# The attention stage's two extra projection weights move to another pool of on-chip memory

## The chip, the cores and the metric

The kernel runs on one core of one Trainium2 chip. The metric is the device time of one execution in microseconds (us), the median of several runs. The core has TensorE (PE in the rows; its weight loads are PEld), VectorE (DVE), ScalarE (ACT), GpSimd (POOL) and SyncE (SP), which issues the DMAs. Every engine takes its instructions in the order in which they stand in its list; semaphores hold an instruction until those it depends on are done.

## The reference

One decoder layer for 4096 prompt positions and 8 single-token samples. Both are projected by one matrix `w_in`; one half of the features goes through a convolution and a gated linear recurrence, the other through windowed attention with sinks. Both halves are gated, joined, and projected by `w_out`.

```python
xn = rms_norm(x, norm_pre)
proj = jnp.einsum('btd,de->bte', xn, w_in)
x_rnn, g_rnn, q, k, v, g_att = jnp.split(proj, SPLITS, axis=-1)
xc, new_conv = causal_conv(x_rnn, conv_state, conv_w, conv_b)
h, h_last = rg_lru(xc, h0, w_gate_a, b_gate_a, w_gate_x, b_gate_x, lru_lambda)
rnn_out = h * jax.nn.silu(g_rnn)
att = window_attention_prompt(q, k, v, attn_sinks, rel_bias)   # the samples: own keys and caches
mix = jnp.concatenate([rnn_out, att * jax.nn.silu(g_att)], axis=-1)
y = x + rms_norm(jnp.einsum('bte,ed->btd', mix, w_out), norm_post)
```

## The kernel before

The positions are cut into eleven chunks: chunk 0 has 256 positions and the 8 samples, chunks 1 to 10 have 384 each. The work goes in three stages. The **recurrent stage** (A) projects every chunk into the recurrence's input and gate (`pr`), forms two gates per block of 128 features on TensorE (`gt`, line 327), runs the scan on VectorE (`hh`, line 352), multiplies it with the SiLU gate (line 361) and stores it into the scratch `mix_d` (line 362). The scan of a chunk needs one square root over all four blocks (`uu`, line 348), for which ScalarE loads another activation table. The **attention stage** (B) projects the chunks again, now to K (`pk`), V (`pv`), four query tiles (`pq`) and four gate tiles (`pga`), each of 24 matmuls, and works through units of one head group and 128 queries: scores (`S`), softmax on VectorE and ScalarE (`tt`, lines 622 to 632), transposes (`pT`), splits (`ph`, `pl`, lines 639 and 640) and products with V (`po`). The **output stage** (C) reads `mix_d` and projects by `w_out`. The products run on values split in two parts (names with h and l), so that three matmuls make one.

**Memory.** Pools are stacked: the attention stage's pools begin where those of the recurrent stage began. The recurrent stage has `pa_late` (bytes 126,592 to 171,136 of each partition: `uu`, `sg`, `aa`, `hh` and others, used until its last instruction), above it `pa` (to 196,896: gate weights, `xk`, `thg`), and above that `prep` (to 220,000: the input rows `xs`). The attention stage has `pb_late` (126,592 to 173,184), `pb` (to 202,848: V `vs`, keys `kt`, softmax `tt`) and `pb1` (to 216,672: `vt`, queries `sq`). The first tile of a new pool that lies over old pools waits until all tiles of the old ones under the pool are released, those that it doesn't touch too; which instruction then carries this wait is seen in the built program.

**Weights.** The attention stage needs ten weight tiles of `w_in`. Eight take the slots of `wpool`; the ninth and tenth, gate tiles 2 and 3 (`wh_in` and `wl_in` 16 and 17), lie at the bottom of `pb_late`. Loading one means a 512 KB DMA into `ws`, a copy on ScalarE (line 111) and a subtraction on VectorE (line 112):

```python
ws = (spare or stage).tile([P, KD, P], F32, tag="ws", name=f"ws_{n}")
nc.sync.dma_start(ws, src)
wh = pool.tile([P, KD, P], F32R, tag="wh", name=f"wh_{n}", bufs=bufs)
act(wh, ws, AF.Copy)
eng.tensor_sub(wl, ws, wh)
```

**Order and PSUM.** The order on every engine is set at build time by a list scheduler that simulates the program and takes what it believes ready first; a wait that falls away or comes up shifts whole stretches. In the attention stage all projections share two PSUM banks (`ps_mm`, line 76); a projection can begin when one of them has been read out. K is read out into `kt` (lines 484, 486), a query tile into `sq` (lines 564 to 567) and, in chunk 0, `qz` (line 571).

Of the kernel before, what the change touches and what calls it, by code (L numbers as in the profile page):

```python
# [9 lines left out]
F32 = mybir.dt.float32  # L10
# [5 lines left out]
P = 128  # L16
# [4 lines left out]
NH = 8  # L21
# [3 lines left out]
NSAMP = 8  # L25
# [19 lines left out]
def hymba_kernel(ctx: ExitStack, tc: tile.TileContext, ins, outs):  # L45
# [69 lines left out]
    def load_w_in(m, pool=None, bufs=None, spare=None, eng=nc.vector, fast=False):  # L115
        return load_w(w_in_v[:, :, m * P:(m + 1) * P], f"in{m}", pool or wpool, bufs, spare, eng, fast)
# [81 lines left out]
    cms = [tc.tile_pool(name=n, bufs=1) for n in ("pa_late", "pa", "prep")]  # L198
# [217 lines left out]
    wB = {}  # L416
# [24 lines left out]
    for ci in range(NCH):  # L441
        for item in A_ORDER:
            f, s = item[0], st[ci]
            c = int(item[1:] or 0)
# [237 lines left out]
    def attend_sample(pool):  # L682
        def window(new, cache, dst, n):
            pr = ps_t(f"pr_{n}")
            nc.tensor.transpose(pr[:NSAMP, 0:P], new, ident)
            row = pbl.tile([NSAMP, P], F32, tag="sh", name=f"row_{n}", bufs=2)
            nc.vector.tensor_copy(row, pr[:NSAMP, 0:P])
            win = pbl.tile([P, NSAMP, P], F32, tag="wh", name=f"win_{n}", bufs=2)
            rows = cache[0].rearrange("b j v d -> j b (v d)")
            nc.sync.dma_start(win[0:112], rows[1:113])  # L690
            nc.sync.dma_start(win[112:P - 1], rows[113:P])
            nc.sync.dma_start(win[P - 1:P], row)
            nc.sync.dma_start(dst[0].rearrange("b j v d -> j b (v d)"), win)
            return win
# [1 line left out]
        kw = window(ksT, ck, o_ks, "k")  # L696
        vw = window(vsT, cv, o_vs, "v")
        yield
        kT = pbl.tile([P, NSAMP, P], F32, tag="wl", name="kT_s", bufs=2)
        for half in range(2):  # L700
            pt = ps_t(f"ptk_{half}")
            for b in range(4):
                nc.tensor.transpose(pt[:, b * P:(b + 1) * P], kw[:, half * 4 + b, :], ident)
            nc.vector.tensor_copy(kT[:, half * 4:half * 4 + 4].rearrange("p b k -> p (b k)"), pt)
        yield
        T = pbl.tile([P, NSAMP, P], F32, tag="wl", name="T_s", bufs=2)[:NH]
        for half, f in enumerate((ps_t, ps_v)):
            S = f(f"S_samp{half}")[:NH].rearrange("p (b k) -> p b k", k=P)
            for b in range(4):
                nc.tensor.matmul(S[:, b, :], qz[:, half * 4 + b, :], kT[:, half * 4 + b, :], start=True, stop=True)  # L710
            nc.vector.tensor_tensor(T[:, half * 4:half * 4 + 4], S,
                                    bs.rearrange("p (o k) -> p o k", o=1).broadcast_to([NH, 4, P]), op=ALU.add)
        m = pool.tile([NH, 4, NSAMP], F32, name="m_s")
        nc.vector.tensor_reduce(m[:, 0], T, axis=mybir.AxisListType.X, op=ALU.max)
        nc.vector.tensor_scalar(m[:, 1], m[:, 0], sk8, None, op0=ALU.max)
        nc.vector.tensor_sub(T, T, m[:, 1].rearrange("p (b o) -> p b o", o=1).broadcast_to([NH, NSAMP, P]))
        act(T, T, AF.Exp)
        nc.vector.tensor_reduce(m[:, 2], T, axis=mybir.AxisListType.X, op=ALU.add)
        act(m[:, 3], m[:, 1], AF.Exp, scale=-1.0, bias=sk8)
# [20 lines left out]
        n = chunks[0][1]  # L740
# [4 lines left out]
    phase[0] = "B"  # L745
    pcms = [tc.tile_pool(name=n, bufs=1, space=bass.MemoryType.PSUM) for n in ("psb0", "psb1", "psb2")]
    ps[:] = [c.__enter__() for c in pcms]
    cms = [tc.tile_pool(name=n, bufs=1) for n in ("pb_late", "pb", "pb1")]
    pbl, pb, pb1 = [c.__enter__() for c in cms]
    xB = load_x(0)  # L750
    for item in B_FIRST:
        if item[0] in "KVQG":
            m = {"K": 12, "V": 13, "Q": 8, "G": 14}[item[0]] + (int(item[1]) if item[0] in "QG" else 0)
            wB[m] = load_w_in(m) if len(wB) < 8 else load_w_in(m, pbl, 2)
    state = [{} for _ in chunks]
    state[0]["xs"] = xB
    work = [chunk_B(ci, state[ci], state[ci - 1]) for ci in range(NCH)]
    for ci in range(NCH):
        for item in B_ORDER if ci else B_FIRST:
            f, args = item[0], [int(i) for i in item[1:]]  # L760
# [10 lines left out]

    wC = [load_w_out(e) for e in range(8)]
    sample = attend_sample(pb)
    turn = 0

    order = [*range(1, NCH), 0]
    for ci in order:
# [14 lines left out]
        for j, (xsrc, ydst, rows, off) in enumerate(tiles):  # L792
            n = f"{ci}_{j}"
# [108 lines left out]
```

## Time and profile before

| | us |
|---|---|
| median of 3 runs (1443.89 to 1446.31) | 1444.59 |
| the profiled execution | 1450.88 |
| its span, first to last instruction | 1449.2 |
| TensorE busy in the span | 1403.5 |
| VectorE, ScalarE, GpSimd busy | 914.3, 800.0, 440.9 |
| last store of the recurrent stage issued | 511.56 |

TensorE is busy nearly without a gap except from 474 to 538 us, where chunk 10 of the recurrent stage and chunk 0 of the attention stage meet. A timeline row gives start, duration, engine, line, operation and operands, with the idle time before it in brackets and what ended it.

### The profile page before, as it was taken

To read this page: it belongs to the slowest core of one execution; us is meant where nothing else is said; L and a number is where in the kernel's file an instruction comes from. 1 tells how busy PE (TensorE), PEld (TensorE's weight loads), DVE (VectorE), ACT (ScalarE), POOL (GpSimd) and SP (SyncE) were. 2 spreads that over 40 slices of the span, in tenths; PEclk is the share of its full clock that TensorE was granted. 3 is DMA by queue.
4 is the path that set the end of the run, shared out by engine and by line. 5 is a ranking of instruction groups with operands and counts; after the bars stand their busy time and mean duration, and the time that the engine had idled before them with its cause. 6 is when DMAs were issued, how large, how long until landed. Compare 5 with 4: busy or idle time off the path is not lost.

```text
span 1449.2 us, 24120 instructions
## 1 busy us (share of the span) xinstructions
PE 1403.5 (97%) x8127; PEld 1323.5 (91%) x8127; DVE 914.3 (63%) x2258; ACT 800.0 (55%) x2055; POOL 440.9 (30%) x876
## 2 busy tenths in 40 slices
PE   5999999999999889999999999999999999999998
PEld 4999989999999779999999999999998888888886
DVE  6778877777777767557566566566784445334433
ACT  4566656665555656577676676576783222222211
POOL 3233332222421033354463453453543000000000
PEclk9999999999999999999999999999999999999999
DMA  9324453434236330330320320330444534433431
GB/s 274 133 83 157 149 168 138 153 131 139 97 121 196 90 117 22 119 106 12 110 99 12 110 99 12 109 99 12 162 133 146 167 134 142 145 133 133 147 129 60
DMA packets 115029, 170.23 MB, mean 117 GB/s; under 512 B 12215, under 2 KB 98823, under 8 KB 114907
## 3 DMA queue, kind: packets, MB, share of 16 engines
q1 hardware_dynamic: 114906, 168.71, 34.7%
q8 instruction: 64, 1.05, 0.3%
q14 instruction: 59, 0.48, 0.1%
HBM read 100.19 MB, written 68.50 MB: 116 GB/s over the span
## 4 chain that ended last, share of the span: by engine, by line
PE 68%; DVE 3%; ACT 2%; DMA 1%; issue 1%; SPq 0%; POOL 0%; POOLq 0%; DVEq 0%; ACTq 0%
PE out L819 8%; PE out L821 8%; PE out L820 8%; PE pga L122 4%; PE pga L123 4%; PE pga L124 4%; PE pq L123 4%; PE pq L122 4%; PE pq L124 4%; PE po L661 3%; PE S L601 2%; PE S L602 2%; PE pT L635 2%; PE pr L122 1%; PE pr L124 1%; PE pr L123 1%
## 5 line engine op out<-in xcount | busy, mean ns | idle before, releaser
L123 PE MATMUL pr<-xl,wh_in 128*128 128x384 f32 (+1 forms) x688 | 231.8, 338 | 0.0
L122 PE MATMUL pr<-xh,wh_in 128*128 128x384 f32 (+1 forms) x688 | 220.1, 340 | 10.8 <-ACT xc L302 10.8
L124 PE MATMUL pr<-xh,wl_in 128*128 128x384 f32 (+1 forms) x688 | 230.0, 336 | 0.0
L819 PE MATMUL out<-wh_out,xh_mix_d 128*128 128x512 f32 (+1 forms) x520 | 201.3, 387 | 0.0
L820 PE MATMUL out<-wl_out,xh_mix_d 128*128 128x512 f32 (+1 forms) x520 | 200.9, 386 | 0.0
L821 PE MATMUL out<-wh_out,xl_mix_d 128*128 128x512 f32 (+1 forms) x520 | 200.5, 386 | 0.0
L838 ACT ACTIVATE sqc<-out 128x512 bf16<-128x512 f32 (+2 forms) x67 | 39.2, 585 | 192.5 <-PE out L821 182.4
L122 PEld LDWEIGHTS pr<-xh,wh_in 128*128 128x128 f32 x688 | 129.9, 191 | 12.5 <-ACT xc L302 12.2
L627 ACT ACTIVATE tt<-tt,nm 128x129 f32<-128x129 f32 x256 | 100.0, 393 | 72.0 <-DVE nm L624 71.8
L841 DVE TENSOR_TENSOR out<-out,gpost 128x512 f32<-128x512 f32 (+1 forms) x65 | 45.4, 699 | 147.6 <-ACT sqc L838 147.0
L123 PEld LDWEIGHTS pr<-xl,wh_in 128*128 128x128 f32 x688 | 131.3, 191 | 0.7 <-issue 0.7
L124 PEld LDWEIGHTS pr<-xh,wl_in 128*128 128x128 f32 x688 | 131.1, 191 | 0.0
L122 PE MATMUL pq<-xh_B,wh_in 128*128 128x384 f32 (+1 forms) x352 | 117.7, 335 | 1.8 <-ACT qz L571 1.1
L123 PE MATMUL pga<-xl_B,wh_in 128*128 128x384 f32 (+1 forms) x352 | 118.8, 337 | 0.0
L122 PE MATMUL pga<-xh_B,wh_in 128*128 128x384 f32 (+1 forms) x352 | 117.7, 334 | 0.7 <-ACT qz L571 0.7
L123 PE MATMUL pq<-xl_B,wh_in 128*128 128x384 f32 (+1 forms) x352 | 118.0, 335 | 0.0
L124 PE MATMUL pq<-xh_B,wl_in 128*128 128x384 f32 (+1 forms) x352 | 117.8, 335 | 0.0
L124 PE MATMUL pga<-xh_B,wl_in 128*128 128x384 f32 (+1 forms) x352 | 117.2, 333 | 0.0
L141 POOL TENSOR_TENSOR rs_c<-ssc,mhalf 128x1 f32<-128x1 f32 (+1 forms) x33 | 20.5, 622 | 315.0 <-DVE ssc L842 276.1
L819 PEld LDWEIGHTS out<-wh_out,xh_mix_d 128*128 128x128 f32 x520 | 97.7, 188 | 19.9 <-issue 0.2
L821 PEld LDWEIGHTS out<-wh_out,xl_mix_d 128*128 128x128 f32 x520 | 97.7, 188 | 19.7
L820 PEld LDWEIGHTS out<-wl_out,xh_mix_d 128*128 128x128 f32 x520 | 97.7, 188 | 19.3
(258 smaller groups left out, 3563.8 us busy)
## 6 DMA issues: line engine op xcount, KB each, us to landing
xs<-in_x_prompt_dram SPq DMA_DIRECT2D x32, 512.0 KB
xr<-in_x_prompt_dram SPq DMA_DIRECT2D x32, 512.0 KB
out_dram<-xr SPq DMA_DIRECT2D x31, 512.0 KB
xT_d<-xh SPq DMA_DIRECT2D x80, 192.0 KB
xT_d<-xl SPq DMA_DIRECT2D x80, 192.0 KB
xf_mix_d<-mix_d SPq DMA_DIRECT2D x80, 192.0 KB
xh_B<-xT_d SPq DMA_DIRECT2D x80, 192.0 KB
xl_B<-xT_d SPq DMA_DIRECT2D x80, 192.0 KB
```

Source lines behind the costliest of these rows:

```text
L122: nc.tensor.matmul(out, wh, xh, start=first, stop=False)
L123: nc.tensor.matmul(out, wh, xl, start=False, stop=False)
L124: nc.tensor.matmul(out, wl, xh, start=False, stop=last)
L601: nc.tensor.matmul(o, qa, kt[:, kv, 0, kr], start=True, stop=False)
L602: nc.tensor.matmul(o, qa, kt[:, kv, 1, kr], start=False, stop=True)
L627: act(tt[:, g, 0:P + 1], tt[:, g, 0:P + 1], AF.Exp, scale=-1.0, bias=nm[:, g:g + 1], accum_out=sm[:, g:g + 1])
L661: nc.tensor.matmul(pog[:, :, r], v.rearrange("p l d -> p (l d)"), w[:, :, r], start=i == 0, stop=i == 2)
L819: nc.tensor.matmul(p, a, wh, start=st, stop=False)
L820: nc.tensor.matmul(p, a, wl, start=False, stop=False)
L821: nc.tensor.matmul(p, b, wh, start=False, stop=sp)
L838: act(sq[:rows, :c[1] - c[0]], p[:rows], AF.Square, scale=1.0 / 32.0, accum_out=ss[:rows, i:i + 1])
L841: nc.vector.tensor_mul(po[i][:rows], p[:rows], gpost[:rows, c[0]:c[1]])
```

## The change

The attention stage opens a fourth pool, `pw`, last, and so on top. The two extra weights move into it, and with them four tiles of the samples' attention in stage C that use the same tags. `pb_late` shrinks by their 16,384 bytes per partition, and everything above it slides down.

```diff
--- before.py
+++ after.py
@@ -685,7 +685,7 @@
             nc.tensor.transpose(pr[:NSAMP, 0:P], new, ident)
             row = pbl.tile([NSAMP, P], F32, tag="sh", name=f"row_{n}", bufs=2)
             nc.vector.tensor_copy(row, pr[:NSAMP, 0:P])
-            win = pbl.tile([P, NSAMP, P], F32, tag="wh", name=f"win_{n}", bufs=2)
+            win = pw.tile([P, NSAMP, P], F32, tag="wh", name=f"win_{n}", bufs=2)
             rows = cache[0].rearrange("b j v d -> j b (v d)")
             nc.sync.dma_start(win[0:112], rows[1:113])
             nc.sync.dma_start(win[112:P - 1], rows[113:P])
@@ -696,14 +696,14 @@
         kw = window(ksT, ck, o_ks, "k")
         vw = window(vsT, cv, o_vs, "v")
         yield
-        kT = pbl.tile([P, NSAMP, P], F32, tag="wl", name="kT_s", bufs=2)
+        kT = pw.tile([P, NSAMP, P], F32, tag="wl", name="kT_s", bufs=2)
         for half in range(2):
             pt = ps_t(f"ptk_{half}")
             for b in range(4):
                 nc.tensor.transpose(pt[:, b * P:(b + 1) * P], kw[:, half * 4 + b, :], ident)
             nc.vector.tensor_copy(kT[:, half * 4:half * 4 + 4].rearrange("p b k -> p (b k)"), pt)
         yield
-        T = pbl.tile([P, NSAMP, P], F32, tag="wl", name="T_s", bufs=2)[:NH]
+        T = pw.tile([P, NSAMP, P], F32, tag="wl", name="T_s", bufs=2)[:NH]
         for half, f in enumerate((ps_t, ps_v)):
             S = f(f"S_samp{half}")[:NH].rearrange("p (b k) -> p b k", k=P)
             for b in range(4):
@@ -745,13 +745,13 @@
     phase[0] = "B"
     pcms = [tc.tile_pool(name=n, bufs=1, space=bass.MemoryType.PSUM) for n in ("psb0", "psb1", "psb2")]
     ps[:] = [c.__enter__() for c in pcms]
-    cms = [tc.tile_pool(name=n, bufs=1) for n in ("pb_late", "pb", "pb1")]
-    pbl, pb, pb1 = [c.__enter__() for c in cms]
+    cms = [tc.tile_pool(name=n, bufs=1) for n in ("pb_late", "pb", "pb1", "pw")]
+    pbl, pb, pb1, pw = [c.__enter__() for c in cms]
     xB = load_x(0)
     for item in B_FIRST:
         if item[0] in "KVQG":
             m = {"K": 12, "V": 13, "Q": 8, "G": 14}[item[0]] + (int(item[1]) if item[0] in "QG" else 0)
-            wB[m] = load_w_in(m) if len(wB) < 8 else load_w_in(m, pbl, 2)
+            wB[m] = load_w_in(m) if len(wB) < 8 else load_w_in(m, pw, 2)
     state = [{} for _ in chunks]
     state[0]["xs"] = xB
     work = [chunk_B(ci, state[ci], state[ci - 1]) for ci in range(NCH)]
```

In the built program the pools now stand so: `pb_late` 126,592 to 156,800, `pb` to 186,464, `pb1` to 200,288, `pw` to 216,672. So `pw` lies over `prep`; but `pb`, which lay over `pa` and the lowest part of `prep`, now begins over `tt`, `aa` and `hh` of `pa_late`, and `pb1` over `xk` and `thg` of `pa`. No instruction is added or taken away; the scheduler writes another order from the end of the recurrent stage on.

ScalarE at the end of the recurrent stage, before: the softmax of the first two units, the copies of the two extra weights, the split of the first unit (`ph`), V's rearranged copies (`vx`). In brackets stand the semaphores waited for (DMAHW: a DMA).

```order
L627 ACTIVATE tt_0_1_5905,sm_0_1_5914<-tt_0_1_5905,nm_0_1_5908 128x129 [waits DVE_49,Pool_49]
L627 ACTIVATE tt_0_1_5905,sm_0_1_5914<-tt_0_1_5905,nm_0_1_5908 128x129 x3
L111 ACTIVATE wh_in_5699<-ws_in_5697 128x1024 [waits DMAHW2_49,DMAHW3_49,DMAHW1_49,DMAHW4_49,DMAHW0_49,DMAHW5_49,DVE_49,Activation_49]
L111 ACTIVATE wh_in_5705<-ws_in_5703 128x1024 [waits DMAHW1_49]
L639 ACTIVATE ph_0_0_5877<-pT_0_0_5872 128x512 [waits PE_49]
L606 ACTIVATE vx_0_1_5898<-vs_1_5741 64x128 [waits Activation_49]
L607 ACTIVATE vx_0_1_5898<-vs_0_5740 64x128
```

The two copies stand ahead of `ph` here. After (`wh_in_5702` and `wh_in_5708` are the same two weights, `vs` and `kt` are V and K of chunk 0):

```order
L111 ACTIVATE wh_in_5702<-ws_in_5700 128x1024 [waits DMAHW0_49]
L337 ACTIVATE tt_2_5537<-thr_2_5533,sp_256 128x384 [waits DVE_49,Activation_49]
L338 ACTIVATE thr_2_5533<-thr_2_5533,sp4n 128x384 [waits Activation_49]
L111 ACTIVATE wh_in_5708<-ws_in_5706 128x1024 [waits DMAHW1_49]
...
L553 ACTIVATE vs_0_5743<-pvt_5740 128x2x64 [waits DMAHW3_49,DMAHW4_49,DMAHW2_49,DMAHW5_49,Activation_49,Pool_49]
L484 ACTIVATE kt_5781<-pk_5782 64x256 x2
```

The copies have moved up to the recurrent stage's `tt` and wait for their own loads alone; the waits for the last stores of `hh` (four DMA semaphores) now stand at the first write of `vs`, behind which stands K's read-out.

VectorE, the scan of chunk 10 (`hh`), before, with softmax rows (`nm`, `ri`, `S`) and query 3's subtractions (`sq`) among it:

```order
L624 TENSOR_TENSOR nm_0_0_5858<-nm_0_0_5858,bneg 128x4 [waits DVE_49]
L566 TENSOR_TENSOR sq_3_6009<-pq_3_5984,sq_3_6009 64x256 [waits PE_49,Activation_49]
L352 SCALAR_TENSOR_TENSOR hh_0_5566<-aa_0_5452,hl_0_5174,thi_0_5448 128x384 [waits DVE_49]
L567 TENSOR_TENSOR sq_3_6009<-pq_3_5984,sq_3_6009 64x256
L352 SCALAR_TENSOR_TENSOR hh_1_5573<-aa_1_5433,hl_1_5181,thi_1_5429 128x384 [waits DMAHW1_49,DVE_49]
L352 SCALAR_TENSOR_TENSOR hh_2_5580<-aa_2_5538,hl_2_5188,thi_2_5534 128x384 [waits DMAHW2_49,DVE_49]
L352 SCALAR_TENSOR_TENSOR hh_3_5587<-aa_3_5557,hl_3_5195,thi_3_5553 128x384 [waits DVE_49]
...
L361 TENSOR_TENSOR hh_1_5573<-hh_1_5573,sg_1_5284 128x384 [waits Pool_49]
L361 TENSOR_TENSOR hh_2_5580<-hh_2_5580,sg_2_5418 128x384 [waits Pool_49]
L361 TENSOR_TENSOR hh_3_5587<-hh_3_5587,sg_3_5524 128x384 [waits Pool_49]
```

Scores and queries stand between the parts of the scan here.

After:

```order
L352 SCALAR_TENSOR_TENSOR hh_0_5566<-aa_0_5452,hl_0_5174,thi_0_5448 128x384 [waits DVE_49]
L352 SCALAR_TENSOR_TENSOR hh_1_5573<-aa_1_5433,hl_1_5181,thi_1_5429 128x384 [waits DVE_49]
L352 SCALAR_TENSOR_TENSOR hh_2_5580<-aa_2_5538,hl_2_5188,thi_2_5534 128x384 [waits DMAHW2_49,DVE_49]
L352 SCALAR_TENSOR_TENSOR hh_3_5587<-aa_3_5557,hl_3_5195,thi_3_5553 128x384 [waits DVE_49]
L361 TENSOR_TENSOR hh_0_5566<-hh_0_5566,sg_0_5351 128x384 [waits Pool_49]
L361 TENSOR_TENSOR hh_1_5573<-hh_1_5573,sg_1_5284 128x384 [waits Pool_49]
L361 TENSOR_TENSOR hh_2_5580<-hh_2_5580,sg_2_5418 128x384 [waits Pool_49]
L361 TENSOR_TENSOR hh_3_5587<-hh_3_5587,sg_3_5524 128x384 [waits Pool_49]
L566 TENSOR_TENSOR sq_1_5841<-pq_1_5816,sq_1_5841 64x256 [waits PE_49,Activation_49]
L567 TENSOR_TENSOR sq_1_5841<-pq_1_5816,sq_1_5841 64x256
L554 SCALAR_TENSOR_TENSOR vs_0_5743<-pvt_5740,vs_0_5743 128x2x64 [waits DMAHW3_49,DMAHW4_49,DMAHW2_49,DMAHW5_49,DVE_49,Activation_49]
L486 SCALAR_TENSOR_TENSOR kt_5781<-pk_5782,kt_5781 64x256 [waits Activation_49]
```

The scan stands in one piece, ahead of query 1's subtractions (`sq_1`), and V's and K's follow.

TensorE behind the last gate product, before (the last rows of query 2's projection `pq_2`, which stands ahead; V's transposes `pvt`; scores; query 3):

```order
L122 MATMUL pq_2_5952<-xh_B_7_5645,wh_in_5675 128x264
L123 MATMUL pq_2_5952<-xl_B_7_5647,wh_in_5675 128x264
L124 MATMUL pq_2_5952<-xh_B_7_5645,wl_in_5676 128x264
L549 MATMUL pvt_5737<-ident,vt_5734 128x128 x2
L601 MATMUL S_0_0_5846<-kt_5778,sq_0_5771 128x128
L601 MATMUL S_0_1_5889<-kt_5778,sq_0_5771 128x256
...
L122 MATMUL pq_3_5984<-xh_B_0_5617,wh_in_5681 128x264
```

Here query 2 and the scores of the first units stand right behind the gates, K's projection far ahead.

After (the last gate products `gt_3`, V's transposes, K's projection `pk`; further down query 2, then the scores):

```order
L122 MATMUL gt_3_5545<-xk_3_5519,gwh 128x384
L123 MATMUL gt_3_5545<-xk_3_5519,gwh 128x384
L124 MATMUL gt_3_5545<-xk_3_5519,gwl 128x384
L549 MATMUL pvt_5740<-ident,vt_5737 128x128 x2
L122 MATMUL pk_5782<-xh_B_0_5620,wh_in_5666 128x264
...
L122 MATMUL pq_2_5955<-xh_B_0_5620,wh_in_5678 128x264
...
L124 MATMUL pq_2_5955<-xh_B_7_5648,wl_in_5679 128x264
L601 MATMUL S_0_0_5849<-kt_5781,sq_0_5774 128x128
```

K's projection, which before stood ahead of and between the gate products, now stands behind the last of them, and query 1 behind it. Query 2 can begin when query 1 has been read out, and the scores stand behind query 2.

## Rows read from the trace of the kernel before

**Rows 1.** The page, part 1: busy us (share of the span) and instructions of each engine.

```profile
PE 1403.5 (97%) x8127; PEld 1323.5 (91%) x8127; DVE 914.3 (63%) x2258; ACT 800.0 (55%) x2055; POOL 440.9 (30%) x876
```

**Rows 2.** Waits of TensorE, 474 to 538 us: waiter <- releaser: us, times, longest.

```profile
PE po L644 <- ACT ph L639: 3.5, 1, 3.5
...
PE pT L635 <- DVE tt L632: 2.2, 1, 2.2
...
PE po L644 <- DVE pl L640: 0.7, 1, 0.7
```

**Rows 3.** Timeline of ScalarE: start, us, engine, line, op, out<-in [idle before <-releaser].

```profile
490.76 0.58 ACT L333 ACTIVATE thr<-gt,hba 128x384 f32<-128x384 f32 x1
...
491.70 0.76 ACT L484 ACTIVATE kt<-pk 64x256 fp32r<-64x256 f32 x2
...
493.23 0.71 ACT L338 ACTIVATE thr<-thr,sp4n 128x384 f32<-128x384 f32 x1
...
495.85 1.28 ACT L348 ACT_TABLE_LOAD   x1
497.14 1.49 ACT L348 ACTIVATE uu<-uu 128x1536 f32<-128x1536 f32 x1
498.65 0.37 ACT L571 ACTIVATE qz<-pq 64x8 f32<-64x8 f32 x2
...
513.65 2.00 ACT L111 ACTIVATE wh_in<-ws_in 128x1024 fp32r<-128x1024 f32 x2 [3.69 <-DMA mix_d<-hh]
515.68 0.60 ACT L639 ACTIVATE ph<-pT 128x512 fp32r<-128x512 f32 x1
```

**Rows 4.** Timeline of VectorE, the same columns.

```profile
486.99 0.55 DVE L313 TENSOR_TENSOR xk<-xc,xk 128x384 fp32r<-128x384 f32 x1
...
489.90 0.43 DVE L567 TENSOR_TENSOR sq<-pq,sq 64x256 fp32r<-64x256 f32 x1
490.36 0.36 DVE L340 TENSOR_SCALAR aa<-thr 128x384 f32<-128x384 f32 x1
...
493.97 0.56 DVE L339 SCALAR_TENSOR_TENSOR thr<-thr,tt 128x384 f32<-128x384 f32 x1 [0.57 <-ACT thr L338]
...
500.25 1.96 DVE L350 TENSOR_TENSOR thi<-thi,uu 128x384 f32<-128x384 f32 x4
...
503.81 1.02 DVE L352 TENSOR_TENSOR_SCAN hh<-aa,hl,thi 128x384 f32<-128x384 f32 x1
...
505.32 2.84 DVE L352 TENSOR_TENSOR_SCAN hh<-aa,hl,thi 128x384 f32<-128x384 f32 x3
...
508.13 0.55 DVE L361 TENSOR_TENSOR hh<-hh,sg 128x384 f32<-128x384 f32 x1
...
510.04 1.49 DVE L361 TENSOR_TENSOR hh<-hh,sg 128x384 f32<-128x384 f32 x3
```

**Rows 5.** The chain that ended last: start, us, what.

```profile
511.56 1.99 DMA mix_d<-hh
```

**Rows 6.** Timeline of TensorE, the same columns as rows 3.

```profile
489.35 0.33 PE L124 MATMUL gt<-xk,gwl 128*128 128x384 f32 x1
...
493.95 0.48 PE L601 MATMUL S<-kt,sq 128*128 128x128 f32 x2
...
495.75 0.28 PE L602 MATMUL S<-kt,sq 128*128 128x256 f32 x1
...
499.74 0.28 PE L122 MATMUL pga<-xh_B,wh_in 128*128 128x264 f32 x1
...
502.62 0.22 PE L601 MATMUL S<-kt,sq 128*128 128x128 f32 x1
...
527.03 0.37 PE L122 MATMUL pq<-xh_B,wh_in 128*128 128x384 f32 x1
```

**Rows 7.** Stretches: us, each engine's busy us (instructions), TensorE's granted clock, DMA share, GB/s.

```profile
480.90:487.90 7.00, 6.27 (x26) 6.28 (x27) 6.23 (x13) 4.57 (x10) 0.00 (x0) 0.51 0.40 120
515.00:522.00 7.00, 4.93 (x19) 4.27 (x20) 4.25 (x8) 6.80 (x24) 0.20 (x1) 0.51 0.01 2
```

## The prediction

> **What bounds the kernel now.** I read the page's part 1 first: TensorE is busy 97% of the span [rows 1], so anything that costs TensorE nothing costs nothing, and anything that makes it idle costs its full length. The waits of TensorE are next: in the stretch where chunk 10 of the recurrence meets chunk 0 of the attention it waits 3.5 us for `ph`, 2.2 us for the softmax, 0.7 us for `pl` [rows 2]. Behind this stretch it has work without a gap, and the instructions are the same ones in both kernels. So the question is one number: at which time does TensorE reach chunk 1's first query matmul, 527.03 us before [rows 6]? What comes later shifts with it.
>
> Why does it wait for `ph`? ScalarE is to see at [rows 3]: the copies of the two extra weights take 2.00 us, the idle 3.69 us ahead of them ends with the DMA of the last `hh`, and `ph` stands right behind them. That DMA began at 511.56 and took 1.99 us, so it landed at 513.55 [rows 5]. The weights lay over the recurrence's buffers. The change takes this wait off them. But the order of ScalarE shows it now at the first write of `vs`, and K's read-out behind it, which ran from 491.70 in the kernel before [rows 3]. Without K there are no scores.
>
> **When the stores land after the change.** The last of the six last gate products started at 489.35 [rows 6], to end near 489.5. K and query 1 no longer stand ahead of it on TensorE, but it reads `xk`, which VectorE had done only at 486.99 + 0.55 = 487.5 [rows 4], so that it can come some 1 us earlier at most. ScalarE gets the two copies (2.00) ahead of it and loses the reads of queries; VectorE loses two subtractions of 0.43 [rows 4] and gains one of the `wl` ones, about as long as a copy. I take 0, within 1 us either way, and count from 489.5, with nothing of the scores in between, as the order of VectorE has it:
>
> - ScalarE: `thr` and `thi` 0.58 each, two reads of query 1 and one of `vt` at some 0.4, `tt` and `thr` 0.71 each [rows 3]: 3.8 less small overlaps, taken as 3.6, to 493.1.
> - VectorE: `thr` 0.56, `aa` 0.36 [rows 4], `uu` taken like `thr`, overlapping a little: to 494.5. The table load, 1.28 [rows 3], lies beside it.
> - The square root, 1.49 [rows 3]: to 496.1. The four `thi` of line 350, 1.96: to 498.0. The scans, 1.02 and 2.84: to 501.9. The multiplications by `sg`, 0.55 and 1.49: to 503.9 [rows 4].
> - The stores, 1.99 [rows 5]: to 505.9. The recurrence thus ends 7.6 us earlier than before, because the scores no longer stand in it.
>
> **Where TensorE stops.** Query 1's subtractions stand behind the scan: 503.9 + 2 x 0.43 = 504.8, and `qz`, 0.37 for both [rows 3], ends at 505.2. Only then is a bank free for query 2. Behind the last gate product TensorE has two transposes, K and query 1, and no more. A projection of 24 matmuls takes 502.62 - 499.74 = 2.88 us [rows 6], 0.12 each. So the work lasts 5.8 us, to 495.3, and TensorE idles some 10 us, to 505.2. In the kernel before it made query 2, scores, query 3 and gates in that time. This is the wait that takes the old one's place; queued behind it on TensorE is all of the attention stage.
>
> **From 505.2 to chunk 1.** The order of TensorE then has six projections (144 matmuls), the first two units' 32 scores, and 20 transposes and products. The scores go at the same pace (16 from 493.95 to near 495.9 [rows 6]). 196 x 0.12 = 23.5 us, which is 528.7 at full clock without a stop. In the kernel before six products with V stand behind the first query matmul at 527.03 that stand ahead of it now, so the fair mark of before is 527.03 + 6 x 0.12 = 527.7. The difference is **+1.0**. Before took 38.2 us from 489.5 to its mark for the same 23.5 us of work, the rest being waits and slow clock, and the new order takes 39.2 with its idle spell and K and query 1; hence the small difference.
>
> **Idle inside that stretch.** Softmax, transposes, splits and products of the first units follow one another as they did. The trace has no row for them in the new order. The upper bound is the whole of the old kind: 2.2 for the softmax plus 0.60 for `ph` plus 0.7 for `pl`, and as much again for the second unit, 6; the lower is 0, since query 3 and a gate tile stand between the scores and the transposes. It can't be less than nothing, for 23.5 has no idle in it. I take one set, **+3.5**, the row of the same operations.
>
> **The clock.** [...]
>
> [...]
>
> **Edits at no cost.** The copies and loads of the extra weights come earlier, ScalarE and SyncE having room there; without that room they would cost their 2.00 us once. GpSimd's first copy into `tt` also waits for the stores; only the softmax, later still, needs it. The shared tags of stage C keep their partners, so nothing new waits there; I bound it by zero on both sides, as its instructions and their order among themselves are the same. The rest of B is shifted by a constant.
>
> **The sum.** 1.0 + 3.5 + 3.1 = +7.6 us; all bounds at their low end give +1.0, at their high end 1.0 + 6 + 5.6 = +12.6. The profiled execution took 1450.88, 6.3 more than the median, of which 1.7 lies outside the span; as no part of that belongs to the change, I put the difference on the median: 1444.59 + 7.6 = 1452.2 (a profiled execution near 1458.5).
>
> **Rivals.**
>
> - *Faster: ScalarE's freed wait decides.* The wait for `ph`, 3.5 [rows 2], and the slow stretch behind it, 2.5, go, and nothing takes their place: 1444.59 - 6.0 = 1438.6. For it speaks that the stores land 7.6 us earlier. It would need the landing before TensorE has run out at 495.3; against it stands a chain of square root, `thi`, scans and multiplications of 1.49 + 1.96 + 3.86 + 2.04 = 9.4 us that cannot begin before 494.6. [...] Chance 0.07.
> - *No change.* The idle is hidden by query 3 and the gate tile, and the clock stays up or the loss is that of before: +1.0, 1445.6. For it: the difference of the two counts is only 1.0. Against: after 10 us without work the rows of before give no case of a clock that stayed. Chance 0.07.
> - *Slower by more.* A second slow stretch and the larger idle: +12.6, 1457.2. For it: the softmax chain repeats for each of the two units, and V's and K's reads on VectorE, 8 of them, stand behind the stores too. Chance 0.2.
> - *The change doesn't do what it says.* The order shows that the copies wait for their own loads alone, so this is left no chance of its own.
>
> **How the numbers follow.** Forecast 0.66, slower by more 0.20, no change 0.07, faster 0.07. About 0.2%, 2.9 us, is what a measurement of this kernel can tell from no change. Faster 0.07, same 0.07, slower 0.86. The range holds the forecast from an idle and clock of about +2.4 in all to the dearer case: 1447.0 to 1457.0. It leaves out the faster case, most of the unchanged one and the top of the dearest.
>
> **What would show it.** In the changed kernel: the weight copies on ScalarE near 485 without idle ahead; the scans on VectorE in one piece, ending near 502, the multiplications near 504; the last `hh` stored near 506, with `vs` and `kt` on ScalarE right behind; TensorE's longest wait at a query (line 122), some 10 us, ended by `qz`; a stretch at 0.51 behind it; chunk 1's first query matmul near 535; stage C shifted whole. I would be wrong if query 2 finds a bank before 500, if the gate products end some us later than 489.5, or if more than one slow stretch follows.

## The result, and the profile after

| | before | after |
|---|---|---|
| median (5 executions each), us | 1444.59 | 1458.84 |
| lowest to highest | 1443.89 to 1446.31 | 1456.83 to 1461.95 |
| ratio | | 1.009 (95%: 1.0074 to 1.0106) |
| profiled execution | 1450.88 | 1456.83 |
| its span | 1449.2 | 1455.1 |
| its mean granted clock of TensorE | 0.991 | 0.987 |

The change makes the kernel slower, by 14.2 us in this first series. The forecast was 1452.2 with a range up to 1457.0; the sign and the place were right, the median lies 1.8 us above the range. Two further series of the changed kernel, each timed beside the kernel before, gave less (1.0062 and 1.0068, below). The profiled executions lie only 5.9 us apart, and that difference between 5.9 and 14.2 is itself one of the things to explain. One execution of the kernel before, 1869.47 us at a granted clock of 0.698, stood far off all others and is left out of every comparison.

In the two profiled executions TensorE is busy equally long, to 0.1 us [rows 1]:

```profile
PE 1403.6 (96%) x8127; PEld 1323.8 (91%) x8127; DVE 914.7 (63%) x2258; ACT 798.2 (55%) x2055; POOL 441.3 (30%) x876
```

So the 5.9 us between these two are idle time; a second trace of the kernel before, below, shows that this does not hold for an ordinary execution. These are TensorE's waits in the stretch (waiter, releaser, us, times, longest). Beside those of [rows 2] the kernel before had one at the gate products:

```profile
PE gt L122 <- ACT thi L334: 3.2, 1, 3.2
```

The changed kernel has, from 474 to 560 us:

```profile
PE pq L122 <- ACT qz L571: 5.9, 1, 5.9
PE gt L122 <- ACT thi L334: 3.9, 1, 3.9
PE gt L122 <- ACT wh_in L111: 2.7, 1, 2.7
PE pT L635 <- DVE tt L632: 1.9, 1, 1.9
PE gt L123 <- DVE xk L313: 1.8, 1, 1.8
PE pvt L549 <- ACT vt L544: 1.4, 1, 1.4
PE po L644 <- ACT ph L639: 1.2, 1, 1.2
PE pT L635 <- ACT tt L627: 0.2, 1, 0.2
```

The wait for `ph` is down from 3.5 to 1.2. In its place stand 5.9 us at query 2, as forecast, and 9.8 us at the gate products and V's transposes, 6.6 more than the 3.2 of before, which were not in the forecast. On ScalarE (start, us, operation, idle before it) the changed kernel has:

```profile
485.21 1.06 ACT L111 ACTIVATE wh_in<-ws_in 128x1024 fp32r<-128x1024 f32 x1 [1.37 <-DMA ws_in<-in_w_in_dram]
...
487.97 0.39 ACT L544 ACTIVATE vt<-pv 128x264 f32<-128x264 f32 x1
...
502.26 0.37 ACT L571 ACTIVATE qz<-pq 64x8 f32<-64x8 f32 x2 [4.67 <-DVE sq L567]
503.37 0.28 ACT L553 ACTIVATE vs<-pvt 128x128 fp32r<-128x128 f32 x1 [0.74 <-DMA mix_d<-hh]
503.54 0.76 ACT L484 ACTIVATE kt<-pk 64x256 fp32r<-64x256 f32 x2
```

The second copy of the extra weights has come forward to 485.21 and waits for its own load; `vs` and `kt` wait for the last store of `hh`, which landed near 503.3. In the kernel before `vt` stood at 473.01; it has gone back by 15 us. Here is the row of before:

```profile
473.01 0.37 ACT L544 ACTIVATE vt<-pv 128x264 f32<-128x264 f32 x1
```

K's projection began behind `vt` in both kernels. These are its first matmuls, before and after:

```profile
474.30 0.28 PE L122 MATMUL pk<-xh_B,wh_in 128*128 128x264 f32 x1
...
488.75 0.57 PE L122 MATMUL pk<-xh_B,wh_in 128*128 128x264 f32 x1
```

VectorE of the changed kernel has the scan in one piece and query 1's subtractions behind it, against [rows 4]:

```profile
493.70 1.96 DVE L350 TENSOR_TENSOR thi<-thi,uu 128x384 f32<-128x384 f32 x4 [1.77 <-ACT uu L348]
495.58 3.74 DVE L352 TENSOR_TENSOR_SCAN hh<-aa,hl,thi 128x384 f32<-128x384 f32 x4
499.24 2.10 DVE L361 TENSOR_TENSOR hh<-hh,sg 128x384 f32<-128x384 f32 x4
501.37 0.42 DVE L566 TENSOR_TENSOR sq<-pq,sq 64x256 fp32r<-64x256 f32 x1
501.80 0.43 DVE L567 TENSOR_TENSOR sq<-pq,sq 64x256 fp32r<-64x256 f32 x1
```

And three stretches (us; busy us and instructions of TensorE, its weight loads, VectorE, ScalarE and GpSimd; granted clock; DMA share; GB/s). First the kernel before from 474 to 489.5:

```profile
474.00:489.50 15.50, 12.27 (x70) 11.92 (x69) 11.29 (x24) 10.56 (x20) 0.00 (x0) 0.78 0.48 143
```

Then the changed kernel, there and up to chunk 1:

```profile
474.00:489.50 15.50, 6.01 (x17) 4.63 (x18) 12.79 (x24) 12.08 (x20) 0.00 (x0) 0.57 0.36 105
...
489.50:502.60 13.10, 7.29 (x47) 7.08 (x45) 10.18 (x18) 5.15 (x10) 3.85 (x4) 0.76 0.15 55
...
502.60:533.70 31.10, 27.75 (x196) 27.04 (x197) 19.57 (x71) 19.02 (x69) 6.17 (x15) 0.88 0.08 23
```

Between the gate products TensorE is busy 6.0 us instead of 12.3. In the kernel before K and query 1, 48 matmuls, stood there. The last stretch holds 196 matmuls, the number that the prediction counted.

### The profile page after: what moved, and what is told of

Same layout as the page of the kernel before. It is cut to its first block, busy times and chain, and to the rows that moved or that the text cites. A ratio compares the mean times of both kernels' runs of the same rounds, so it can differ in the third digit from the quotient of the medians.

```text
span 1455.1 us, 24121 instructions
## 1 busy us (share of the span) xinstructions
PE 1403.6 (96%) x8127; PEld 1323.8 (91%) x8127; DVE 914.7 (63%) x2258; ACT 798.2 (55%) x2055; POOL 441.3 (30%) x876
## 4 chain that ended last, share of the span: by engine, by line
PE 68%; ACT 3%; DVE 2%; DMA 1%; issue 0%; POOL 0%; POOLq 0%; DVEq 0%; ACTq 0%; SPq 0%
PE out L819 8%; PE out L820 8%; PE out L821 8%; PE pga L123 4%; PE pga L122 4%; PE pga L124 4%; PE pq L123 4%; PE pq L122 4%; PE pq L124 4%; PE po L661 3%; PE S L601 2%; PE S L602 2%; PE pT L635 2%; PE pr L122 1%; PE pr L124 1%; PE pr L123 1%
```

## The experiments

Every ratio is to the kernel before, timed beside the same runs, with its 95% interval.

### The kernel before again

No edit.

> The kernel before, unchanged, to see how its executions differ from each other. The changed kernel is 14.2 us above it by the medians, while its profiled execution is only 5.9 us longer (span 1455.1 against 1449.2), and the stretch from the last recurrent projection to the steady part of the attention stage grew by 7.6 us. [...] Rival (elsewhere): the clock is 0.991 in ordinary executions too, and the 6.3 us lie in waits of the recurrent stage. [...]

Measured: ratio 1.0004 (0.9992 to 1.0015), 1445.6 us, profiled execution 1445.81 with clock 0.994, twelve executions from 1442.78 (clock 0.995) to 1450.31 (0.990). Eight of the twelve have a clock of 0.994 or 0.995, and slower work is most of the difference in time: on the same instructions TensorE is busy 1399.7 us here, at a clock of 0.994, and was busy 1403.5 in the first profiled execution [rows 1], at 0.991, which is 3.8 of the 5.1 us by which the spans differ.

```profile
PE 1399.7 (97%) x8127; PEld 1319.5 (91%) x8127; DVE 913.3 (63%) x2258; ACT 800.1 (55%) x2055; POOL 439.6 (30%) x876
```

The first profiled execution, at 1450.88, was a dear one. That settles the gap of the two differences: of the 8.3 us between 14.2 and 5.9, before's profiled execution lay 6.3 above its median, and after's 2.0 below its own. Measured against this second trace the changed kernel's span is 11.0 us longer, of which 3.9 are busy time and 7.1 idle. Where the first execution's 5.1 us of span went can be read from two marks, the first matmul of V's projection and the first query matmul of chunk 1. In this execution:

```profile
447.14 0.28 PE L122 MATMUL pv<-xh_B,wh_in 128*128 128x264 f32 x1
...
521.83 0.37 PE L122 MATMUL pq<-xh_B,wh_in 128*128 128x384 f32 x1
```

From V to chunk 1 that is 74.7 us. In the first profiled execution V began at

```profile
450.77 0.28 PE L122 MATMUL pv<-xh_B,wh_in 128*128 128x264 f32 x1
```

and it was 527.03 [rows 6] - 450.77 = 76.3 us. So 3.6 us of the difference were lost ahead of V, in the recurrent stage, where the rival had put them, and 1.6 in the stretch that the change touches. Of the two low stretches of [rows 7] the first was shorter here: 479.00 to 482.00 is at 0.50, and over the 15.5 us that answer to 474 to 489.5 (3.6 us earlier here) the clock is 0.89 instead of 0.78, with the same waits but for 0.3 us:

```profile
470.40:485.90 15.50, 11.51 (x72) 10.98 (x71) 12.35 (x26) 10.85 (x22) 0.44 (x3) 0.89 0.49 145
...
479.00:482.00 3.00, 3.00 (x15) 3.00 (x15) 3.00 (x9) 2.54 (x5) 0.00 (x0) 0.50 0.52 150
```

### The pool alone

```diff
-    cms = [tc.tile_pool(name=n, bufs=1) for n in ("pb_late", "pb", "pb1", "pw")]
-    pbl, pb, pb1, pw = [c.__enter__() for c in cms]
+    cms = [tc.tile_pool(name=n, bufs=1) for n in ("pb_late", "pw", "pb", "pb1")]
+    pbl, pw, pb, pb1 = [c.__enter__() for c in cms]
```

> The fourth pool is kept, but opened second, so that every tile of the attention stage lies at its address of the kernel before. The copies of the extra weights wait for the last stores again and K's and V's read-out does not. Theory (slide): what costs is that V and K slid over the recurrence's last buffers; this kernel is the kernel before, ratio 1.000 within 0.2%. Rival (pool): the pool of its own costs by itself, through another order of instructions; then it stays near 1.009.

Measured: 1.001 (0.9998 to 1.0022), 1446.27 us. A pool of its own costs nothing that can be told from none; the addresses do. This holds for the slide as a whole, and does not say which of the slid pools it is.

### K, V and the weights out of the way of the last stores

```diff
-    pbl, pb, pb1, pw = [c.__enter__() for c in cms]
+    pbl, pbt, pad, pb, pb1, pw = [c.__enter__() for c in cms]
+    pad.tile([P, 1936], F32, name="pad_")
...
-            tt = pb.tile([P, 4, 130], F32, tag="tt", name=f"tt_{n}", bufs=3)
+            tt = pbt.tile([P, 4, 130], F32, tag="tt", name=f"tt_{n}", bufs=3)
```

The pools are opened in the order of these names (`pb_late` is `pbl`); `nm`, `sm` and `ri` move to `pbt` in the same way.

> The changed kernel, but the softmax tiles have a pool of their own right above the late one, and 7.7 KB are left unused behind it, so that keys, values, queries and extra weights all begin above the recurrence's last buffers. Neither the copies nor the read-out of K and V wait for the last stores; only V's rearranged copies and the softmax do. Theory (slide): the 10 us without work on TensorE go, 13 to 20 us less than the changed kernel, ratio 0.996 to 1.000 (1438 to 1445 us). Rival (order): the order that the scheduler writes, with the scan in one piece and K behind the gates, is what costs; then the ratio stays above 1.004.

Measured: 1.008 (1.0061 to 1.0098), 1456.51 us. This felled the reason that I had put first. K and V no longer wait for a store, and the time is that of the changed kernel. TensorE's waits from 474 to 545 us say where to look:

```profile
PE gt L122 <- ACT thi L334: 3.8, 1, 3.8
PE gt L122 <- ACT wh_in L111: 2.7, 1, 2.7
...
PE gt L123 <- DVE xk L313: 1.8, 1, 1.8
PE pvt L549 <- ACT vt L544: 1.4, 1, 1.4
```

They are the waits ahead of 489.5, the same to 0.1 us as in the changed kernel, with K and query 1 behind the gates as there. In this kernel `pb1`, which holds `vt` and the queries, still lies over the recurrence's gate rows. `vt` is the first tile of it that is written, so it carries the wait for the last `xk`, and the read-outs of query 0 stand behind it on ScalarE. Until then V's projection and query 0 hold the only two PSUM banks for projections, and K cannot begin. That is the theory of the banks: in the traces `vt` is written at 488.02 here and K begins at 488.81.

### One edit to the kernel before: the queries' pool lower

```diff
-    cms = [tc.tile_pool(name=n, bufs=1) for n in ("pb_late", "pb", "pb1")]
-    pbl, pb, pb1 = [c.__enter__() for c in cms]
+    cms = [tc.tile_pool(name=n, bufs=1) for n in ("pb_late", "pb1", "pb")]
+    pbl, pb1, pb = [c.__enter__() for c in cms]
```

This raises the pool of K, V and the softmax above the queries' pool by as much as that one's size; it still begins above the recurrence's last buffers.

> The kernel before, its extra weights where they were, but the pools of the attention stage opened in the order late, pb1, pb: V's transposed copy and the queries now lie over the recurrence's input rows xk and wait for their last use, as in the changed kernel; K and V lie above them and wait for no store, the weight copies wait for the stores as before. Theory (banks): V's projection holds one of the two PSUM banks until vt may be written and query 0 the other, so K and query 1 cannot start between the gate products; this alone makes TensorE idle there and brings the clock down, ratio 1.006 to 1.011. Rival (stores): what costs is K's read-out waiting for the last stores; that wait isn't here, and the ratio is 1.000 within 0.2%.

Measured: 1.0087 (1.0067 to 1.0106), 1459.24 us. The weights are where they were, no read-out of K or V waits for a store, and the whole loss is there. The waits:

```profile
PE pT L635 <- DVE tt L632: 7.2, 1, 7.2
PE gt L122 <- ACT thi L334: 3.8, 1, 3.8
PE gt L122 <- DVE xk L312: 3.5, 1, 3.5
PE S L601 <- DVE sq L566: 3.1, 1, 3.1
```

and from 474 to 489.5 TensorE is busy 9.3 us at a clock of 0.56:

```profile
474.00:489.50 15.50, 9.28 (x37) 8.09 (x38) 10.81 (x25) 11.32 (x21) 0.44 (x3) 0.56 0.23 68
```

### One edit to the changed kernel: the queries' pool back on top

```diff
-    cms = [tc.tile_pool(name=n, bufs=1) for n in ("pb_late", "pb", "pb1", "pw")]
-    pbl, pb, pb1, pw = [c.__enter__() for c in cms]
+    cms = [tc.tile_pool(name=n, bufs=1) for n in ("pb_late", "pb", "pw", "pb1")]
+    pbl, pb, pw, pb1 = [c.__enter__() for c in cms]
```

> The changed kernel, with the weights' pool opened third instead of last, so that vt and the queries lie where they lay before, over the finished input rows, and wait for nothing of the recurrence; K's and V's read-out still waits for the last stores, and the weight copies don't. Theory (banks): K and query 1 stand between the gate products again, and most of the loss goes: ratio 0.998 to 1.004, what is left being K's bank, held until the stores land near 506, and the scores behind it. Rival (stores): the loss stays, 1.007 or more.

Measured: 1.0022 (1.0011 to 1.0033), 1449.99 us. With `vt` and the queries free again, and K and V still waiting for the stores, most of the loss is gone. From 474 to 489.5 TensorE is as busy as in the kernel before:

```profile
474.00:489.50 15.50, 11.99 (x76) 11.20 (x75) 11.82 (x24) 11.73 (x23) 0.00 (x0) 0.89 0.40 118
```

What is left are waits for banks behind the gates, while K's bank is held:

```profile
PE pga L122 <- ACT qz L571: 3.5, 1, 3.5
PE pq L122 <- ACT qz L571: 2.9, 2, 2.3
```

### Everything early

early_high, with one more gap, so that `pb1` begins at 197,024, above the gate rows:

```diff
-    pbl, pbt, pad, pb, pb1, pw = [c.__enter__() for c in cms]
+    pbl, pbt, pad, pb, pad2, pb1, pw = [c.__enter__() for c in cms]
+    pad2.tile([P, 704], F32, name="pad2_")
```

> The changed kernel with the softmax tiles in a pool right above the late one, and two unused gaps, so that K and V begin above the recurrence's last buffers, and vt, the queries and the weights above its input rows. No copy and no read-out that TensorE needs waits for the recurrence's last stores or for xk. Theory (banks): the order between the gates is that of the kernel before, the 3.5 us for ph go, and with them some of the slow clock: 2 to 7 us less than before, ratio 0.995 to 0.9985. Rival (another order costs again, or the softmax takes the place of ph as the latest): 1.000 within 0.2%. By the rival of the stores, which blames what early_high had removed already, it cannot be better than early_high, 1.008.

Measured: 1.0006 (0.9993 to 1.0019), 1447.62 us. From early_high to here only the place of the queries' pool and of the weights' above it differs, and 0.0074 of the ratio go. From pb1_top to here, with the store wait of K and V gone, it is 2.4 us, but the two intervals overlap. Yet the gain over the kernel before that I expected isn't there; the rival, no change within 0.2%, holds. The 3.5 us for `ph` are gone from the waits, and others have come:

```profile
PE pga L122 <- ACT qz L571: 3.7, 1, 3.7
PE gt L122 <- ACT thi L334: 3.1, 1, 3.1
```

ScalarE shows why:

```profile
503.76 0.37 ACT L571 ACTIVATE qz<-pq 64x8 f32<-64x8 f32 x2 [5.38 <-DVE sq L567]
507.92 0.31 ACT L606 ACTIVATE vx<-vs 64x128 fp32r<-64x128 f32 x1 [3.79 <-DMA mix_d<-hh]
```

Query 3 is read out only when VectorE has its subtractions done, which now stand behind the scan, and ScalarE waits 3.79 us for the same last store as before, at V's rearranged copies `vx`, which lie in the late pool. The 3.69 us of [rows 3] have moved to another instruction.

### One bank instead of two

all_early, with `vt` alone over the gate rows, in a pool of its own under `pad2`:

```diff
-    pbl, pbt, pad, pb, pad2, pb1, pw = [c.__enter__() for c in cms]
+    pbl, pbt, pad, pb, pvt_, pad2, pb1, pw = [c.__enter__() for c in cms]
...
-    pad2.tile([P, 704], F32, name="pad2_")
+    pad2.tile([P, 320], F32, name="pad2_")
...
-            vt = pb1.tile([P, STEP], F32, tag="vt", name=f"vt_{ci}", bufs=1)
+            vt = pvt_.tile([P, STEP], F32, tag="vt", name=f"vt_{ci}", bufs=1)
```

> all_early, with V's transposed copy vt alone moved down over the recurrence's gate rows, so that it waits for the last xk as in the changed kernel; queries, K, V and the weights wait for nothing of the recurrence that matters. Theory (banks): V's projection now holds one of the two banks through the gates, query 0's is free; K stands between the third and the last gate's products, query 1 behind the last. One bank held instead of two gives part of the loss: 3 to 9 us over all_early (1.0006), ratio 1.002 to 1.007. Rival (the queries' wait is what counts): ratio as all_early, below 1.002.

Measured: 1.0016 (1.0004 to 1.0028), 1447.81 us, below what the theory asked for and not to be told from all_early. So the result is the rival's: V's bank held alone costs little, if anything, since query 0's bank lets K in between the gates. It does not tell whether the whole loss needs both banks held or only the queries' wait; no run lowers the queries without `vt`, and this stays open.

### The idle time filled

```diff
+    W0 = chunks[0][1] + chunks[0][2]
...
+            if ci == 0 and item == "Q1":
+                dm = ps_t("dummy")
+                for k in range(48):
+                    nc.tensor.matmul(dm[:, :W0], wB[12][0][:, k % KD, :], xB[0][k % KD], start=True, stop=True)
```

> The changed kernel with 48 matmuls added whose result nobody reads (K's weights times the input, into a PSUM bank that is free there): 19 stand behind the last gate product, 29 behind query 1, in the time in which TensorE has no work. They add 5.8 us of work at full clock. Theory (clock): part of the loss is that the idle spell lowers the clock for the work behind it; with the spell filled the clock is up when query 2 begins, and the time falls by 2 to 4 us although work was added: ratio 1.006 to 1.0075. Rival (idle alone): the clock costs nothing that the waits don't hide; the time stays within 1 us of the changed kernel, 1.009, or grows.

Measured: 1.0043 (1.0026 to 1.006), 1451.96 us. With 5.8 us of work added the changed kernel is 2 to 7 us faster (1458.84, 1453.94 and 1455.16 without). The interval overlaps those of the second and third series without the work (from 1.0045 and 1.0052), so the size of the gain is uncertain; from V to chunk 1 the trace has 80.4 us against 83.8 to 84.7 in three traces without it. The first row is from inside the slow stretch, the second from there on to 538 us:

```profile
478.60:492.00 13.40, 7.21 (x27) 6.33 (x28) 10.86 (x21) 10.50 (x19) 0.00 (x0) 0.50 0.20 60
492.20:538.00 45.80, 42.99 (x324) 41.42 (x324) 30.73 (x91) 24.77 (x83) 10.67 (x21) 1.00 0.27 93
```

The clock stays up from 492 on, where the changed kernel still has two slow stretches, and the wait at query 2 is 0.4 instead of 5.9, the added work standing in its place.

The scheduler also moved some scores forward, so not all of the gain need be the clock's.

The same trick in kernels with less idle time gave nothing that could be measured. This is added to the kernel before, and to all_early as well:

```diff
             if first:
+                for i in range(32 if kv == 0 else 0):
+                    nc.tensor.matmul(po[:, 0:2 * P], wB[12][0][:, i % KD, :],
+                                     wB[12][1][:, 0:2, :].rearrange("p k c -> p (k c)"), start=True, stop=True)
```

> The kernel before with 32 matmuls added whose result is overwritten (into the bank of the first product with V, ahead of it): 3.8 us of work among the scores of the second head group, ahead of the waits for the softmax (2.2) and ph (3.5), which take them up. [...] Rival (work): the added work is not all covered; 1 to 3 us more, ratio 1.0005 to 1.002.

Measured: 1.0001 (0.9986 to 1.0017), 1446.61 us, below the rival's range, and no gain either. The trace shows that the experiment did not do what was meant: the 32 matmuls run from 499.70 to 503.7, and behind them, where there had been waits of 2.2 for the softmax and 3.5 for `ph`, stands one wait of 7.1 for `ph`, up to 515.57, with the clock at 0.50 from 514 to 518. The added time is covered, but the idle time was gathered and not filled, so this run says nothing on what filling it would give.

> all_early with the same 32 matmuls; here they stand behind gate tile 0, where TensorE waited 3.7 us for query 3 to be read out. Theory (clock): they cost nothing and keep the clock up, 1 to 4 us less than all_early (1.0006): ratio 0.998 to 1.000. Rival: that wait brought the clock down in too few executions to matter; ratio as all_early, within 0.1%.

Measured: 0.9995 (0.9984 to 1.0007), 1445.83 us, clock 0.996. Inside the expected range, but its interval holds no change; that it beats the kernel before is not shown. Here too a wait remains behind the added work, 3.8 us for `nm` up to 508.71.

### The changed kernel again, twice

No edit.

> The changed kernel, unchanged, for a second trace and more executions. If the 14.2 us between the medians are the change's own, the ratio is 1.008 to 1.010 again and the mean granted clock of the executions lies near 0.987, all below those of the kernel before. Rival (the first measurement happened to fall high): ratio 1.004 to 1.007, near the 5.9 us between the first two profiled executions.

Measured: 1.0062 (1.0045 to 1.008), 1453.94 us, executions from 1452.25 to 1458.94 at clocks of 0.987 to 0.990. The rival holds: the first series had fallen high.

> The changed kernel once more, since its first median lay 14.2 us above before's and its second 8.1. Theory (clock): nothing but the clock of the single execution differs; the executions of all three series lie on one line of time against mean granted clock, near 1.3 to 1.7 us for each 0.001, those of this series between 0.985 and 0.990, and the ratio falls between 1.005 and 1.010. Rival (two levels): the series differ by more than their clocks; then executions at the same clock differ by over 4 us between the series.

Measured: 1.0068 (1.0052 to 1.0084), 1455.16 us, from 1454.11 to 1456.14 at 0.988 to 0.990. The first series had clocks of 0.985 to 0.988. At like clocks the series differ by less than the 4 us of the rival, though at one place barely (3.9): at 0.987 the first has 1456.83, 1457.65 and 1459.38, the second 1458.94; at 0.988 the first has 1458.84, the third 1456.14 and 1454.91. Taken together the 17 executions of the changed kernel have a median of 1455.4 at a mean clock of 0.988, the 96 of the kernel before that were timed with these runs 1445.7 at 0.993. So the change costs near 9.7 us; the three series, each against the kernel before beside it, gave 14.2, 8.1 and 10.0. The runs after the first result were made on four chips, and why the first series had the lowest clocks is not known.

The marks of a second trace of the changed kernel agree with the first:

```profile
448.52 0.28 PE L122 MATMUL pv<-xh_B,wh_in 128*128 128x264 f32 x1
...
532.32 0.34 PE L122 MATMUL pq<-xh_B,wh_in 128*128 128x384 f32 x1
```

83.8 us from V to chunk 1. In the first trace it is 533.72 - 448.98 = 84.7:

```profile
448.98 0.28 PE L122 MATMUL pv<-xh_B,wh_in 128*128 128x264 f32 x1
...
533.72 0.34 PE L122 MATMUL pq<-xh_B,wh_in 128*128 128x384 f32 x1
```

## Where the prediction was right, and where it failed

**The stage, right in size.** The forecast put chunk 1's first query matmul at 528.7 + 3.5 + 3.1 = 535.3, which is 8.3 us behind before's 527.03. Measured from V's first matmul, so that the recurrent stage drops out, it is 84.74 - 76.26 = 8.5 between the two profiled executions.

**Its steps.** The landing of the stores was forecast for 505.9; V was read at 503.37, which with the 1.8 us that this execution was ahead at V is 505.2. The reading of query 1 was forecast to end at 505.2, and ended at 502.26 + 0.37 = 502.6, or 504.4 with the same shift. The copies stand near 485 as forecast, but wait 1.37 for their load. The idle behind it, forecast at 3.5, is 1.9 + 1.2 + 0.2. The clock was to take 3.1 behind query 2. That was my estimate, half of the 6.27 us busy in the first stretch of [rows 7], as the 2.5 of the faster rival is half of the 4.93 in the second and 5.6 is both together; no run shows that an idle spell is paid for with one such stretch. What was measured: 31.1 us for 196 matmuls are 23.5 at full pace, 3.3 of idle and 4.3 of the rest, of which 3.5 are slow clock by the same reckoning (half of the 4.0 and 3.0 us busy in two stretches at 0.50). These terms hold within 1.5 us each.

**Ahead of query 2, wrong twice, in opposite directions.** I let TensorE do K and query 1 in 5.8 us behind the last gate and idle 10. It idled 9.8 us earlier already, at the gates and `vt`, the clock was 0.50 there, from 476.5 to 493.0, K took 5.0 us for its 24 matmuls (from 488.75 to 493.75) instead of 2.88, and 5.9 us were left to wait. As VectorE's chain, the scan and query 1's subtractions behind it, sets the end of this wait, the sum didn't notice; that it came out right here was luck.

**The cause, wrong.** I took the order as given and laid the loss on K's read-out waiting for the last stores. early_high, without that wait, is as slow (1.008); pb1_low, the kernel before with the queries' pool lowered below K's and V's, is as slow too (1.0087); pb1_top, which keeps the wait for the stores, is not (1.0022). What moves K behind the gates is the place of `vt` and the queries over `xk` and `thg`; that much the runs show. That it acts through the two held PSUM banks fits the rows (K begins 0.9 us behind the end of the copy into `vt` in the kernel before and 0.4 us in the changed one), but vt_low, made to test it, came out as the rival said, and the queries alone were not tried. The store wait is the smaller part, some 2 us by pb1_top. The parts don't add up to the change, whose waits lie beside each other.

**The base and the range, wrong.** These are the steps on which the forecast missed. The first is the base. I counted the +7.6 against the profiled execution of before, put it on the median, and set the 6.3 us between the two aside as no part of the change. But 1.6 of them lay in the changed stretch. Against the second trace of before, 74.7 us from V to chunk 1, the three traces of the changed kernel, 83.8 to 84.7, are 9.1 to 10.0 longer and not 8.3. That agrees with the 9.7 us of all executions, which on the median of before is 1454.3 and inside the range.

The second is the clock, with which the rest goes. I gave it one value, with bounds of 0 to 5.6, in one place; two slow stretches came behind query 2, 500.3 to 506.7 and 520.7 to 523.7, where more than one was named as a sign of being wrong. Above all the range had no share for what the clock does from one execution to the next. Among those of before, 1443.4 us is the median at 0.995 and 1448.5 at 0.992; among those of after, 1454.1 at 0.990 and 1458.3 at 0.987, that is, 1.3 to 1.6 us for each 0.001 by straight lines through either set. The first series, at 0.985 to 0.988, lies 3.4 us above the median of all 17. A range for the median of five executions should have reached some 3 us further up.

How much of the 9.7 us is clock can't be read from the mean clocks, since these count slow spells in which TensorE mostly waits (from 476.5 to 488.5 the changed kernel is at 0.50 and TensorE busy for 5.0 of 12.0 us). Its busy time, on the same instructions, is 1399.7 us in the second trace of before and 1403.6, 1402.2 and 1402.2 in those of the changed kernel: 2.5 to 3.9 us are slower work, and the other 6.5 to 7.1 us of the spans are idle time.

**The faster rival.** The wait for `ph` was removed, and removing it gains nothing even in all_early, where no read-out that TensorE needs waits for the recurrence's last buffers: 1.0006. What comes late next is VectorE's scan, which ends the wait under another name. The kernel before shows VectorE busy for 22.07 of 24.05 us (third figure of the busy times):

```profile
489.50:513.55 24.05, 17.54 (x136) 16.22 (x134) 22.07 (x70) 14.37 (x39) 2.99 (x8) 1.00 0.10 34
```

The changed kernel's trace is at 0.50 at each of its three idle spells from 474 to 538. The first slow stretch begins inside the wait of 3.9 us at the gate products, which ends at 477.58, and lasts through the other waits at the gates and `vt` and through K's projection up to 493.0; the second begins inside the wait of 5.9 at query 2, which ends at 502.69; the third begins 0.7 us behind the end of the waits of 1.9 and 1.2, at 520.01:

```profile
476.50:493.00 16.50, 9.51 (x33) 8.13 (x34) 13.53 (x27) 13.36 (x23) 0.00 (x0) 0.50 0.22 64
...
500.30:506.70 6.40, 4.01 (x18) 4.02 (x19) 3.23 (x8) 3.56 (x13) 0.89 (x4) 0.50 0.35 125
520.70:523.70 3.00, 3.00 (x15) 3.00 (x16) 3.00 (x14) 0.18 (x2) 0.00 (x0) 0.50 0.00 0
```

The forecast had one stretch where there are three. Its term came near all the same, since the slow time behind query 2, 3.5 us, is close to the 3.1 of one stretch, and the stretch ahead of it cost nothing more at query 2, where 5.9 us of waiting were left.

## What to carry to other kernels

When pools slide, list for each new tile which old tiles it comes to lie over, and ask of the first one that is written whether it gives back a scarce buffer, here a PSUM bank: small copies that wait can hold up a whole projection two steps away (K began at 488.75 here instead of 474.30). A wait that is removed is worth only the distance to the next one (the 3.5 us for `ph` brought nothing in all_early, 1.0006); look for the engine that is busy right through the stretch (VectorE, 22 of 24 us here) before counting on it. Where a kernel's idle time is bunched, time several executions with their clocks before costing anything on one profile, and give the clock a share of the range.

## What the runs showed of the hardware

Executions of one unchanged kernel differed by 8.4 us within one series on one chip (1443.70 to 1452.07) and by 10.5 over all series and chips (1441.54 to 1452.07), and the mean granted clock goes with it (0.995 to 0.989). Work that nobody needs, put where TensorE had waited 5.9 us at query 2, went with a kernel 2 to 7 us faster and a clock of 1.00 behind it. In the two kernels with waits of 2 to 4 us the added work did not land in the waits, so whether filling such waits pays is not shown.
